# Keeping the second FFN's low weight halves in DRAM between its two passes

## The chip, the cores and the metric

One core of one Trainium2 chip runs the whole program. The metric is the time of one execution in device microseconds (us); the kernel before takes 3142.2 us, the median of three runs (3121.45 to 3152.75).

## The reference

Two layers of a decoder run over 1024 tokens of width 1024, float32. Layer 0 mixes tokens with an S5 state space model and differential attention, layer 1 with RWKV-7. Each layer ends in a gated SwiGLU FFN of hidden width 2816, and these two FFNs are what the change is about:

```python
def swiglu(h, w_gate, w_up, w_down):
    return (jax.nn.silu(h @ w_gate) * (h @ w_up)) @ w_down

for l in range(DEPTH):                       # DEPTH = 2
    ...
    h = rms_norm(x, norm_ffn[l]) * (1.0 + scale_f) + shift_f
    x = x + gate_f * swiglu(h, ffn_w_gate[l], ffn_w_up[l], ffn_w_down[l])
```

## The kernel before

The 1024 tokens are two blocks of 512 (`TB`). Each FFN makes one pass over block 0 and one over block 1, and each pass reads all three weight matrices. A pass (`ffn`, line 516) goes through the hidden width in six chunks of 3, 3, 4, 4, 4 and 4 slabs of 128 columns (`CHUNKS`, line 47). For each slab there is a gate tile and an up tile of 128x1024 (512 KB); then, for the chunk, eight down tiles d0 to d7 of 128x384 (192 KB) or 128x512 (256 KB). TensorE takes 24 matmuls of 512 columns for a gate or an up tile, and 9 or 12 for a down tile.

Each operand of these matmuls is split into a rounded high half and the rest, the low half. For a weight tile this is `wsplit` (line 443): the raw tile is loaded (line 448), ScalarE casts it to the high half (451), and the low half is raw minus high, on VectorE (457) or, when `eng` is GpSimd, there in pieces of 256 columns (464). With `key` given, the low half is instead stored to DRAM by the first pass (`flush_lo`, line 469, at the next `wsplit`) and loaded by the second (453):

```python
        nc.scalar.copy(hi, raw)
        if key in self.los:
            nc.sync.dma_start(lo.bitcast(F32), self.los.pop(key))
            return hi, lo
        self.flush_lo()
        if eng is None:
            nc.vector.tensor_tensor(lo, raw, hi.bitcast(F32), op=ALU.subtract)
        ...
        if key is not None:
            self.unsaved = key, lo, shape
```

Raw, high and low tiles have two buffers each (pool `wp`, line 182). So the high or the low half of a tile can be written only when TensorE has done with the tile two before it, while a raw tile can come as soon as its two readers have done. For each slice of 128 rows, `mm3g` (line 483) issues three matmuls: high weights by high activations, high by low, low by high. The first matmul that needs a low half is thus the third of its tile. Down tiles have one peculiarity (lines 564 to 567): d0 and d1 both run all but their last slice, then d0 and d1 finish one right behind the other, then d2 to d7 follow in turn.

The passes stand in `run` (line 1772) beside other work. Layer 0's pass over block 0 runs beside attention, with VectorE's subtraction, and stores its low halves; its pass over block 1 runs beside the RWKV algebra of block 0 and loads them. Layer 1's pass over block 0 runs beside the algebra of block 1 with the subtraction on GpSimd (`pool`, lines 1835 and 1839), its last chunk's down tiles after the output projection `rwkv_wo`. Layer 1's pass over block 1 (lines 1843 to 1848) comes last and runs alone, but for the transposes and stores of the output (`store_x`); there VectorE subtracts. TensorE's order is fixed by the program (`manual_schedule`, line 1790). The other queues, SyncE's DMA queue among them, are ordered by a scheduler, and each executes strictly in that order.

Of the kernel before, what the change touches and what calls it, by code (L numbers as in the profile page):

```python
# [18 lines left out]
P = 128  # L19
D = 1024  # L20
S = 1024
KT = D // P
# [67 lines left out]
def chain(*gens):  # L90
    for g in gens:
        yield from g


def lockstep(*gens):

    gens = list(gens)
    while gens:
        for g in gens[:]:
            if next(g, gens) is gens:  # L100
                gens.remove(g)
        yield
# [44 lines left out]
class Trunk:  # L147
# [368 lines left out]
    def ffn(self, l, st, chunks, eng=None, parts="ud", dtag="B"):  # L516

        nc, A = self.nc, self.A
        wg, wu, wd = A["ffn_w_gate"][l], A["ffn_w_up"][l], A["ffn_w_down"][l]
        gate = self.mod[l][:, 40:48]  # L520
        tp, x = self.tp, st["x"]
        hh, hl = st["h"]
        if "d" not in st:
            st["d"] = [self.page([P, 4, TB], F32R, "dd", dtag) for _ in range(2)]
        dd = st["d"]
        for f0, f1 in chunks:
            nf = f1 - f0
            for f in range(f0, f1) if "u" in parts else ():
                yield from next(self.inject, ())
                pp, gens = [], []  # L530
                for w, nme in ((wg, "pg"), (wu, "pu")):
                    hi, lo = self.wsplit(
                        w[:, f * P : (f + 1) * P].rearrange("(k p) n -> p k n", p=P), [P, KT, P], eng, None if l else (nme, f)
                    )
                    pt = self.ps.tile([P, TB], F32, tag="mm", name=self.nm(nme))
                    g = self.mm3w(pt, hi, lo, hh, hl, KT)
                    if f:
                        yield from g
                    gens.append(g)
                    pp.append(pt)  # L540
                if not f:
                    yield from lockstep(*gens)

                sg = tp.tile([P, TB], F32, tag="t0", name=self.nm("sg"))
                nc.scalar.activation(sg, pp[0], AF.Tanh, scale=0.5)
                nc.vector.scalar_tensor_tensor(sg, sg, 1.0, pp[0], op0=ALU.add, op1=ALU.mult)
                hd = tp.tile([P, TB], F32, tag="t1", name=self.nm("hd"))
                nc.vector.scalar_tensor_tensor(hd, pp[1], 0.5, sg, op0=ALU.mult, op1=ALU.mult)
                nc.scalar.copy(dd[0][:, f - f0, :], hd)
                nc.vector.tensor_tensor(dd[1][:, f - f0, :], hd, dd[0][:, f - f0, :].bitcast(F32), op=ALU.subtract)  # L550
            if "d" in parts:

                def down(n):
                    hi, lo = self.wsplit(
                        wd[f0 * P : f1 * P, n * P : (n + 1) * P].rearrange("(k p) n -> p k n", p=P), [P, nf, P], eng,
                        None if l else (f0, n),
                    )
                    pd = self.ps.tile([P, TB], F32, tag="mm", name=self.nm("pd"))
                    yield from self.mm3w(pd, hi, lo, dd[0], dd[1], nf)
                    nc.vector.scalar_tensor_tensor(x[:, n, :], pd, gate[:, n : n + 1], x[:, n, :], op0=ALU.mult, op1=ALU.add)  # L560
                    if l == 0 and f1 == NF:
                        self.square(x[:, n, :], n)

                d0, d1 = down(0), down(1)
                yield from self.some(d0, nf - 1)
                yield from self.some(d1, nf - 1)
                yield from chain(d0, d1, *(down(n) for n in range(2, KT)))
# [1350 lines left out]
```

## Time and profile before

| | us |
|---|---|
| median of three runs | 3142.2 (3152.75, 3142.2, 3121.45) |
| the profiled execution's own time | 3132.61 |
| its span, first to last instruction | 3130.8 |
| layer 1's algebra of block 1, with most of the FFN pass over block 0 | 2066 to 2640 |
| output projection, last down tiles of block 0 | 2640 to 2730 |
| layer 1's FFN pass over block 1, output stores | 2730 to 3131 |

Times in the trace count from the span's start. The page gives the busy time of each engine; idle time of an engine counts only where the end of the span hangs on it. A matmul's busy time overlaps that of the next one, so the spacing of matmul starts tells more than their durations. The granted TensorE clock is 1.00 at 2.4 GHz.

### The profile page before, as it was taken

The page shows a single profiled execution, that of the slowest core. Times are in us where ns is not written, and L with a number is a line of the kernel's source. Part 1 is how long each engine was busy: PE and PEld are TensorE (multiplying, and loading weights), DVE is VectorE, ACT ScalarE, POOL GpSimd, SP SyncE. Part 2 cuts the span into 40 slices and gives each one's busy share as a digit, 9 for nine tenths or more (in the row PEclk, how much of TensorE's full clock was granted, in tenths as well). Part 3 has the DMA queues.
Part 4 walks back from the last instruction along what each step waited for, and adds up shares of the span by engine and source line. Part 5 has one row for each costly group of instructions (what it writes and reads, how often), then busy time and mean ns, then how long its engine had stood idle before and what let it go on. Part 6 is the DMA issues. An engine that isn't in the chain of part 4 may idle for free.

```text
span 3130.8 us, 51897 instructions
## 1 busy us (share of the span) xinstructions
PE 2891.5 (92%) x19582; PEld 2232.2 (71%) x19582; DVE 1852.6 (59%) x3886; ACT 1219.5 (39%) x2542; POOL 787.4 (25%) x1127
## 2 busy tenths in 40 slices
PE   4879998998899999999999999989999999999999
PEld 1668866776677767677777777667777778777777
DVE  6854655556574744677777336467778773444443
ACT  3212444333322644454544236444444443322222
POOL 6552501001110300122221112035455545300000
PEclk7889999999999999999999999999999999999999
DMA  7764222546786445434434564422222223523333
GB/s 247 196 148 75 71 75 84 158 130 207 232 285 196 158 140 155 133 110 138 127 119 138 166 197 134 155 88 79 69 68 85 73 77 111 167 86 90 101 102 93
DMA packets 532746, 411.90 MB, mean 132 GB/s; under 512 B 47225, under 2 KB 474513, under 8 KB 531473
## 3 DMA queue, kind: packets, MB, share of 16 engines
q1 hardware_dynamic: 517168, 378.16, 40.2%
q0 software_dynamic: 7632, 25.68, 2.6%
q10 hardware_dynamic: 7696, 4.74, 0.5%
q8 instruction: 156, 2.56, 0.3%
q14 instruction: 94, 0.76, 0.1%
HBM read 331.42 MB, written 77.07 MB: 130 GB/s over the span
## 4 chain that ended last, share of the span: by engine, by line
PE 72%; DVE 12%; DMA 8%; ACT 4%; issue 3%; POOL 1%; SPq 0%; ACTq 0%; DVEq 0%; POOLq 0%
PE pu L489 14%; PE pg L489 14%; PE pd L489 12%; PE pkrv L489 8%; PE pout L489 5%; PE pq L489 4%; DMA mwt<-in_w_ada 2%; DVE wlo L457 2%; DMA ks<-kd 1%; PE sps L1027 1%; DMA wraw<-in_ffn_w_gate 1%; ACT whi L451 1%; DVE FS L1509 1%; PE pA L1536 1%; DMA wlo<-wld 1%
## 5 line engine op out<-in xcount | busy, mean ns | idle before, releaser
L451 ACT CAST whi<-wraw 128x1024 fp32r<-128x1024 f32 (+2 forms) x472 | 402.0, 852 | 934.9 <-PE pu L489 203.6
L457 DVE TENSOR_TENSOR wlo<-wraw,whi 128x1024 fp32r<-128x1024 f32 (+2 forms) x288 | 297.6, 1033 | 297.5 <-ACT whi L451 285.8
L489 PE MATMUL pd<-dd,whi 128*128 128x512 f32 x1408 | 458.4, 407 | 15.1 <-DVE x L560 10.6
L489 PE MATMUL pg<-fhi,whi 128*128 128x512 f32 x704 | 296.7, 421 | 22.4 <-ACT whi L451 13.0
L489 PEld LDWEIGHTS pd<-dd,whi 128*128 128x128 f32 x1408 | 251.8, 188 | 79.2 <-ACT whi L451 19.9
L489 PE MATMUL pu<-fhi,whi 128*128 128x512 f32 x704 | 291.9, 415 | 2.3 <-ACT ev L1393 1.6
L489 PE MATMUL pd<-dd,wlo 128*128 128x512 f32 x704 | 279.5, 397 | 8.5 <-DMA wlo<-wld 8.2
L489 PE MATMUL pg<-fhi,wlo 128*128 128x512 f32 x704 | 282.1, 401 | 2.9 <-DVE wlo L457 2.6
L489 PE MATMUL pu<-fhi,wlo 128*128 128x512 f32 x704 | 278.9, 396 | 2.6 <-DVE wlo L457 1.5
L489 PE MATMUL pg<-flo,whi 128*128 128x512 f32 x704 | 280.3, 398 | 0.0
L489 PE MATMUL pu<-flo,whi 128*128 128x512 f32 x704 | 277.5, 394 | 0.0
L464 POOL TENSOR_TENSOR wlo<-wraw,whi 128x256 fp32r<-128x256 f32 (+1 forms) x272 | 203.6, 777 | 217.4 <-ACT whi L451 212.2
L560 DVE SCALAR_TENSOR_TENSOR x<-pd,mod,x 128x512 f32<-128x512 f32 x192 | 143.5, 748 | 138.8 <-PE pd L489 137.8
L489 PE MATMUL pkrv<-xh,whi 128*128 128x512 f32 x384 | 164.9, 429 | 15.9 <-ACT ev L1393 11.2
L489 PEld LDWEIGHTS pg<-fhi,whi 128*128 128x128 f32 x704 | 134.3, 191 | 58.7 <-ACT whi L451 15.5
L489 PEld LDWEIGHTS pd<-dd,wlo 128*128 128x128 f32 x704 | 132.4, 188 | 48.5 <-DMA wlo<-wld 12.3
L489 PEld LDWEIGHTS pg<-fhi,wlo 128*128 128x128 f32 x704 | 134.2, 191 | 38.1 <-DVE wlo L457 6.2
L489 PEld LDWEIGHTS pu<-fhi,whi 128*128 128x128 f32 x704 | 132.8, 189 | 35.6 <-ACT ev L1393 2.5
L489 PEld LDWEIGHTS pu<-fhi,wlo 128*128 128x128 f32 x704 | 132.6, 188 | 34.1 <-DVE wlo L457 2.0
L489 PE MATMUL pkrv<-xh,wlo 128*128 128x512 f32 x384 | 154.9, 403 | 1.7 <-DVE wlo L457 1.7
L489 PE MATMUL pkrv<-xl,whi 128*128 128x512 f32 x384 | 154.2, 402 | 0.0
L489 PEld LDWEIGHTS pg<-flo,whi 128*128 128x128 f32 x704 | 134.7, 191 | 24.8
(460 smaller groups left out, 5933.5 us busy)
## 6 DMA issues: line engine op xcount, KB each, us to landing
wraw<-in_ffn_w_gate SPq DMA_DIRECT2D x88, 512.0 KB, 3.8
wraw<-in_ffn_w_up SPq DMA_DIRECT2D x88, 512.0 KB, 4.0
wraw<-in_ffn_w_down SPq DMA_DIRECT2D x128, 256.0 KB, 2.7
mwt<-in_w_ada POOLq DMA_DIRECT2D x48, 512.0 KB, 6.1
wld<-wlo SPq DMA_DIRECT2D x44, 512.0 KB, 3.1
wlo<-wld SPq DMA_DIRECT2D x44, 512.0 KB, 3.3
mwt<-in_w_ada SPq DMA_DIRECT2D x32, 512.0 KB, 5.9
wraw<-in_ffn_w_down SPq DMA_DIRECT2D x64, 192.0 KB, 2.4
```

What stands on the lines that cost most here:

```text
L451: nc.scalar.copy(hi, raw)
L457: nc.vector.tensor_tensor(lo, raw, hi.bitcast(F32), op=ALU.subtract)
L464: eng.tensor_tensor(o, a, h, op=ALU.subtract)
L489: nc.tensor.matmul(out, lhsT=w(k), rhs=x(k), start=first and i == 0, stop=last and i == n - 1)
L560: nc.vector.scalar_tensor_tensor(x[:, n, :], pd, gate[:, n : n + 1], x[:, n, :], op0=ALU.mult, op1=ALU.add)
L1027: nc.tensor.matmul(sp[:, c0 : c0 + n], lhsT=qT[r : r + 64, hd, o : o + P], rhs=kT[r : r + 64, hd % 2, c0 : c0 + n], start=True, stop=c0 + ...
L1509: v.scalar_tensor_tensor(FS[r, :, o : o + 64], c8(x)[r], 0.5 if x is bt else 1.0, c8(Wi)[r], op0=M, op1=M)
L1536: nc.tensor.matmul(pas[h][:, c, :], lhsT=FS[rows[h], c, :], rhs=AR[h][rows[h], c, :], start=True, stop=True)
```

## The change

The condition that kept layer 1 from having a key goes, and the layer number enters the key. Layer 1's pass over block 0 now stores each low half that GpSimd has computed; its pass over block 1 loads it instead of having VectorE subtract.

```diff
@@ ffn, gate and up tiles
-                        w[:, f * P : (f + 1) * P].rearrange("(k p) n -> p k n", p=P), [P, KT, P], eng, None if l else (nme, f)
+                        w[:, f * P : (f + 1) * P].rearrange("(k p) n -> p k n", p=P), [P, KT, P], eng, (l, nme, f)
@@ ffn, down tiles
-                        None if l else (f0, n),
+                        (l, f0, n),
```

TensorE's, GpSimd's and (but for two pairs of neighbours) ScalarE's instructions keep their order. VectorE loses 91 subtractions. The SyncE queue gains 92 stores and 91 loads. On it, at the down tiles of the last pass's first chunk, there stood before only raw loads (wraw, line 448), each behind VectorE's last reading of the raw tile two before:

```order
L448 DMA wraw_28421<-in_ffn_w_down 128x3x128 [waits DMAHW2_49,DVE_49]
L448 DMA wraw_28434<-in_ffn_w_down 128x3x128 [waits DMAHW3_49,DVE_49]
L448 DMA wraw_28455<-in_ffn_w_down 128x3x128 [waits DMAHW4_49,DVE_49]
L448 DMA wraw_28480<-in_ffn_w_down 128x3x128 [waits DMAHW5_49,DVE_49]
L448 DMA wraw_28497<-in_ffn_w_down 128x3x128 [waits DMAHW6_49,DVE_49]
```

At the same place now each raw load is followed by a load of a low half (wlo, line 453) from its DRAM copy (wld):

```order
L448 DMA wraw_28616<-in_ffn_w_down 128x3x128 [waits DMAHW3_49,Activation_49]
L453 DMA wlo_28606<-wld_20794 128x384 [waits DMAHW4_49,PE_49]
L448 DMA wraw_28637<-in_ffn_w_down 128x3x128 [waits DMAHW5_49,Activation_49]
L453 DMA wlo_28619<-wld_20875 128x384 [waits DMAHW6_49,PE_49]
L448 DMA wraw_28662<-in_ffn_w_down 128x3x128 [waits DMAHW7_49,Activation_49]
L453 DMA wlo_28640<-wld_20920 128x384 [waits DMAHW0_49,PE_49]
L448 DMA wraw_28679<-in_ffn_w_down 128x3x128 [waits DMAHW1_49,Activation_49]
```

The load of a low half waits for TensorE (PE), which must have done with the tile two before, and the raw loads now wait for ScalarE alone. In the pass over block 0, beside the algebra, the same queue had raw loads that wait for GpSimd (Pool) between the algebra's own loads and stores (ks, rr, wa, RV, g2w, zd):

```order
L448 DMA wraw_21496<-in_ffn_w_gate 128x8x128 [waits DMAHW7_49,Activation_49,Pool_49]
L1767 DMA zd<-yq_20918 128x2x128 [waits DMAHW5_49,DVE_49]
L1460 DMA ks_21395<-kd 128x2x128 [waits DMAHW6_49,DVE_49]
L448 DMA wraw_21627<-in_ffn_w_up 128x8x128 [waits DMAHW1_49,Activation_49,Pool_49]
L448 DMA wraw_21785<-in_ffn_w_gate 128x8x128 [waits DMAHW0_49,DMAHW4_49,Activation_49,Pool_49]
```

Now a store stands directly ahead of each of these raw loads and has taken over its wait for GpSimd:

```order
L473 DMA wld_21379<-wlo_21224 128x1024 [waits DMAHW2_49,Pool_49]
L448 DMA wraw_21526<-in_ffn_w_gate 128x8x128 [waits DMAHW4_49,DMAHW3_49,Activation_49]
L1767 DMA zd<-yq_20936 128x2x128 [waits DVE_49]
L1460 DMA ks_21425<-kd 128x2x128 [waits DMAHW5_49,DVE_49]
L473 DMA wld_21531<-wlo_21377 128x1024 [waits DMAHW6_49,Pool_49]
L448 DMA wraw_21659<-in_ffn_w_up 128x8x128 [waits DMAHW7_49,Activation_49]
```

The order of the algebra's transfers among the raw loads is the same as before. Since `flush_lo` stores a tile only at the next `wsplit` that computes one, the last tile of block 0 is stored under a key that the last tile of block 1 has already asked for: that one tile is still subtracted on VectorE, and its store is not used.

## Rows read from the trace of the kernel before

**Rows 1.** The page: busy time of the engines; TensorE's granted clock by slice.

```profile
PE 2891.5 (92%) x19582; PEld 2232.2 (71%) x19582; DVE 1852.6 (59%) x3886; ACT 1219.5 (39%) x2542; POOL 787.4 (25%) x1127
...
PEclk7889999999999999999999999999999999999999
```

**Rows 2.** Busy time by stage: window, length, engines (instructions), clock, DMA share, GB/s.

```profile
1228.00:1841.00 613.00, 586.76 (x5221) 448.19 (x5220) 387.67 (x1048) 274.70 (x700) 117.34 (x175) 0.99 0.45 137
2066.00:2640.00 574.00, 542.87 (x5047) 416.04 (x5046) 415.26 (x1031) 256.27 (x666) 293.54 (x411) 1.00 0.27 78
...
2730.00:3131.00 401.00, 385.01 (x1654) 304.09 (x1652) 166.30 (x219) 101.34 (x144) 0.00 (x0) 0.99 0.32 95
```

**Rows 3.** TensorE's groups, 2730 to 3131: busy, mean ns, idle before and its releaser.

```profile
L489 PE MATMUL pd<-dd,whi 128*128 128x512 f32 x356 | 113.7, 400 | 3.4 <-DVE x L560 2.2 <-DVE xo L373 1.2
L489 PE MATMUL pg<-fhi,wlo 128*128 128x512 f32 x176 | 70.7, 401 | 1.1 <-DVE wlo L457 1.1
...
L489 PE MATMUL pu<-fhi,wlo 128*128 128x512 f32 x176 | 70.1, 398 | 1.5 <-DVE wlo L457 1.5
```

**Rows 4.** VectorE's costliest group, 2730 to 3131.

```profile
L457 DVE TENSOR_TENSOR wlo<-wraw,whi 128x1024 fp32r<-128x1024 f32 (+2 forms) x92 | 84.6, 920 | 99.2 <-ACT whi L451 98.5
```

**Rows 5.** Timeline (start, length, what), last pass, first chunk: d2's subtraction and start.

```profile
2775.18 0.55 DVE L457 TENSOR_TENSOR wlo<-wraw,whi 128x384 fp32r<-128x384 f32 x1
2775.41 0.71 PE L489 MATMUL pd<-dd,whi 128*128 128x512 f32 x2 [0.24 <-DVE x L560]
```

**Rows 6.** Timeline, layer 0, block 1, last chunk: down tiles' loads (SPq) and matmuls.

```profile
1821.26 0.33 SPq L453 DMA_DIRECT2D wlo<-wld  x1
...
1824.92 0.50 PE L489 MATMUL pd<-dd,wlo 128*128 128x512 f32 x1 [1.15 <-DMA wlo<-wld]
...
1827.54 0.32 SPq L453 DMA_DIRECT2D wlo<-wld  x1
...
1828.44 0.70 PE L489 MATMUL pd<-dd,whi 128*128 128x512 f32 x2 [0.24 <-DVE x L560]
...
1830.36 0.50 PE L489 MATMUL pd<-dd,wlo 128*128 128x512 f32 x1 [1.22 <-DMA wlo<-wld]
...
1835.80 0.32 SPq L453 DMA_DIRECT2D wlo<-wld  x1
...
1838.89 0.40 PE L489 MATMUL pd<-dd,wlo 128*128 128x512 f32 x1
```

**Rows 7.** DMA issues, 1228 to 1841: count, KB each, median us to landing.

```profile
wlo<-wld SPq DMA_DIRECT2D x44, 512.0 KB, 3.3
...
wlo<-wld SPq DMA_DIRECT2D x31, 256.0 KB, 2.8
...
wlo<-wld SPq DMA_DIRECT2D x16, 192.0 KB, 2.4
...
ks<-kd SPq DMA_DIRECT2D x14, 128.0 KB, 4.0
```

**Rows 8.** Timeline, layer 0, block 1, fifth chunk: d6, gate load behind it.

```profile
1763.86 0.33 SPq L453 DMA_DIRECT2D wlo<-wld  x1
...
1764.32 0.45 SPq L448 DMA_DIRECT2D wraw<-in_ffn_w_gate  x1
...
1768.67 0.50 PE L489 MATMUL pd<-dd,wlo 128*128 128x512 f32 x1 [1.56 <-DMA wlo<-wld]
```

**Rows 9.** What the SyncE queue waited for, 2066 to 2640: total us, times, longest.

```profile
SPq L448 <- POOL wlo L464: 132.4, 67, 3.4
```

**Rows 10.** DMA issues, 2066 to 2640.

```profile
ks<-kd SPq DMA_DIRECT2D x14, 128.0 KB, 2.3
```

**Rows 11.** TensorE by stretch: window, length, busy (matmuls), granted clock, DMA share, GB/s.

```profile
2050.00:2053.50 3.50, 1.41 (x7) 1.00 0.02 9
2053.50:2057.30 3.80, 3.80 (x13) 0.55 0.93 265
...
1815.00:1831.00 16.00, 13.39 (x56) 1.00 0.57 172
```

## The prediction

> **What bounds the kernel now.** I read the page first, then the busy time by stage, then in the last stage TensorE's groups with their idle time, and last the timeline at single tiles. The page shows TensorE busy 92% of the span, its clock full outside the first slices [rows 1]. By stage, the last pass (2730 to 3131) is TensorE's alone: 385.01 us busy of 401 while VectorE has 166.30 and GpSimd nothing [rows 2]. The reader is to see there that VectorE, whose 92 subtractions go (84.6 us, [rows 4]), is not what the end waits for. TensorE's idle time that names the low half is 1.1 us before gate and 1.5 us before up matmuls, and none before down matmuls [rows 3]. So at most 2.6 us can be gained where work is taken away. The stage in which work is added, the algebra with the pass over block 0, is also TensorE's: 542.87 of 574 us [rows 2].
>
> The question is therefore whether a load can be as punctual as the subtraction was. The subtraction of a down tile takes 0.55 us and follows the cast at once; when d2 starts at 2775.41 its low half is all but there [rows 5]. A load takes 2.4 us for 192 KB, 2.8 for 256 KB and 3.3 for 512 KB from issue to landing [rows 7]. It can't be issued earlier than the subtraction could start, because the buffer it writes is the one that TensorE leaves free two tiles before.
>
> **The change part by part.** One matmul per 0.233 us is the unit (385.01 us for 1654, [rows 2]). Layer 0's pass over block 1 already does what the change asks of layer 1, and near its end, when the algebra thins out, it runs about as dense as the last pass will. I take the prices there.
>
> *Down tiles in a row, d3 to d5.* With four slices, a load is issued at 1835.80 and the third matmul of its tile comes at 1838.89 without a wait [rows 6]: the cover is 3.09 us against 2.8. This is the matmul time of one tile (12 x 0.233 = 2.80) plus two matmuls less the issue. With three slices the cover is three matmuls shorter, 3.09 - 0.70 = 2.39, against 2.4. Price: nothing. If that cover is gone because a load lands 0.4 us later, 0.4 us on every second tile, some 3 us in all.
>
> *Gate and up tiles in a row.* The cover is 24 matmuls, 5.6 us plus 0.3, against 3.3. Nothing; it would take a landing beyond 5.9 us.
>
> *From up to down tiles, six times.* d1's buffer is left by the last up tile, and only d0's nine matmuls lie between; d2's is left by d0, and only d1's last slice lies between. The rows show both waits: 1.15 us at 1824.92 for the load issued at 1821.26 (landing 3.66 us), and 1.22 us at 1830.36 for that of 1827.54 (2.82 us) [rows 6]. The 0.24 us on VectorE's residual ahead of d2 is there in both kernels [rows 5, 6], so it doesn't count. In the last pass there is less other traffic. At 2.8 us d1 would wait only 2.8 - 2.37 (9 + 2 matmuls less 0.2) = 0.43. So a turn costs between 1.65 and 2.37 us; I take 1.9, nearer to the median landing. With three slices d1 has 0.70 less cover and both loads land 0.4 sooner: 0.73 + 0.82 = 1.55, about the same. Six turns: 6 x 1.9 = 11.4 us (9.3 to 14.2).
>
> *From down to gate tiles, five times.* The raw gate and up tiles of 512 KB come in beside the low halves of d6, d7 and gate. The row has d6's load issued at 1763.86, the gate tile right behind at 1764.32, and TensorE waiting 1.56 us until 1768.67: a landing of 4.81 us [rows 8]. The gate's own low half needs 3.3 us where d7 covers 3.09: 0.2. With three slices the gate's cover is 2.39: 0.9. Three turns of 1.8 and two of 2.5 are 10.3 us. The lower bound takes the median landings for all (0.2 and 0.9: 2.4 us), the upper 4.81 us for two loads of each turn (twice 1.72 and twice 2.42: 20 us).
>
> *First gate and up pair.* They run in lockstep, so the up tile's load has five matmuls (1.2 us) of cover against 3.3: some 2.3 us, where 1.5 us went on the subtraction: +0.8 (0 to 2).
>
> *Removed.* The gate matmuls' 1.1 us [rows 3] goes; the up tile's 1.5 is counted above. VectorE's 84.6 us free nothing else, since it is idle most of that stage.
>
> *Stores in the pass over block 0.* 92 stores of 34.6 MB (44 of 512 KB, 32 of 256, 16 of 192) over some 650 us are about 53 GB/s on top of 78, under the 137 of the stage that loads them in layer 0 [rows 2]. On the SyncE queue a store waits for GpSimd's subtraction; queued behind it are the next raw load and the algebra's ks, rr, wa and RV loads, for which VectorE, ScalarE and TensorE wait. But the raw load at that place waited for the same GpSimd instruction before (132.4 us in 67 waits, [rows 9]), so the queue stands no longer than it did. GpSimd must now also wait for a store before it writes that buffer again, but that is two tiles later. What is left is traffic ahead of the ks loads: they land in 2.3 us here [rows 10] and in 4.0 us in the stage where low halves are loaded [rows 7]. Sixteen times 1.7 us, all of it exposed, is 27 us, the upper bound; below, -1. I take +2, near the side of nothing, because that layer 0 stage has its loads held up by queue entries that wait for TensorE, which the stores don't.
>
> *Last tile.* It is still subtracted, and its store of 256 KB is not on the path: nothing.
>
> Sum: 11.4 + 10.3 + 0.8 - 1.1 + 2 = +23.4 us, which is 3132.6 + 23.4 = 3156.0 on the profiled execution. That execution is 9.6 us below the median of the three runs shown. The mean of all four times is 3137.3, and from it I forecast 3160.7 us, rounded 3161.
>
> The rows say one more thing of such waits. Where TensorE was busy only 1.41 of 3.50 us, the granted clock fell to 0.55 (from 2.4 towards 1.2 GHz) over the next 3.8 us; in the 16 us that hold the two waits of rows 6 it stayed 1.00 [rows 11]. The Trainium skill, "TensorE: Matmul & The Clock Gate", section "HAM oscillation — how this bites in real kernels", describes a kernel whose DMA wait between short groups of matmuls throttles the clock anew each time. By that rule every turn would pay a stretch at half clock; by the row of the nearest case none would. It is a rival below.
>
> **The rivals.**
>
> *Hidden after all (-3 to +8 us).* The landings of rows 6 and 8 were stretched by the algebra's own transfers; alone, d1 waits 0.4 us, and the turns to gate almost nothing. Against it: d2's 1.22 us came with a plain landing of 2.82 us, so six of these (7.3 us) remain. About 3142 us.
>
> *Every down tile late, slower than before.* In the last pass the traffic roughly doubles from 95 GB/s [rows 2], and if the down tiles' loads land in 4.81 us throughout, as d6's did [rows 8], the cover fails on every second tile, as a late tile lengthens its successor's cover. Sixteen of the 32 four-slice tiles by 1.72 and eight of the 16 three-slice ones by 2.42 are 46.9; with +0.8 - 1.1 + 2 that is +48.6, 3186 us. It decides from a landing of about 3.2 us on. For it: 4.81 was seen. Against: no wait at the tiles of 1831 to 1841.
>
> *The clock falls at the turns, slower.* If each of the 11 turns is followed by 3.8 us at 0.55, each costs 3.8 x 0.45 = 1.7 us, 18.8 more: +42, 3179 us. For it: the fall after the gap at 2050. Against: the full clock across the two waits of rows 6.
>
> *The algebra's loads suffer, slower.* The upper bound of the stores: +23.4 - 2 + 27 = +48, 3186 us. Against: the wait that the store takes over.
>
> *The change doesn't do what it says.* The key could miss; but the queue shows 91 loads and VectorE 91 subtractions fewer, so only the last tile misses. No chance of its own.
>
> **How the numbers follow.** Within 1% means within 31 us of 3137, about what a measurement of this kernel can tell from no change. My forecast has 0.54, of which 0.43 lie under +31 and 0.11 above. Hidden after all has 0.17, every tile late 0.17, the clock 0.06, the algebra's loads 0.04. Something that makes TensorE faster than its 2.6 us of removable waits allow has 0.02. Slower: 0.11 + 0.17 + 0.06 + 0.04 = 0.38; same: 0.43 + 0.17 = 0.60; faster 0.02. The range leaves out the bottom of the hidden case and the tail above +56: 3136 to 3193. The forecast's own range, from its terms' bounds without the algebra's 27 us, is 3147 to 3178 (9.3 + 2.4 + 0 - 1.1 - 1 = 9.6 above 3137.3, and 14.2 + 20 + 3 + 2 - 1.1 + 2 = 40).
>
> **What would show it.** In the changed kernel's profile, TensorE's idle time before down matmuls with the low half should name the load (wlo from wld) with 12 to 20 us in the last pass, in two waits of about 1 us at d1 and d2 of each chunk, and the gate matmuls should name it with 1 to 5. VectorE's subtraction keeps one instruction there. The granted clock stays 0.99 or 1.00, and the pass over block 0 takes the same time within 3 us. I am wrong if d3 to d5 wait too, if the clock falls behind the turns, if ks lands near 4 us and the stage from 2066 grows, or if TensorE doesn't wait for the loads at all.

## The result, and the profile after

The changed kernel takes 3160.41 us, the median of 20 runs (3142.47 to 3168.86), against 3137.41 us of 20 runs of the kernel before on the same chip. The ratio is 1.0071, 95% interval 1.0059 to 1.0083: 19 to 26 us slower, and by the bound of 1% no change. The forecast was 3161 us.

The profiled execution took 3150.99 us, its span 3149.1. That is 18.3 us over the profiled one before, a little under the interval, so a few of the timed microseconds have no place in the pair of traces.

The page of the changed kernel answers to [rows 1]. VectorE has 91 instructions and 77.6 us fewer, and TensorE has 12 us more busy time for the same 19582 instructions. The down matmuls with the low half, of both layers together, waited 8.2 us for loads before, all in layer 0's pass over block 1, and wait 14.8 now.

```profile
PE 2903.3 (92%) x19582; PEld 2236.4 (71%) x19582; DVE 1775.0 (56%) x3795; ACT 1219.6 (39%) x2542; POOL 788.2 (25%) x1127
...
PEclk7889998999999999999999999999999999999999
...
L457 DVE TENSOR_TENSOR wlo<-wraw,whi 128x1024 fp32r<-128x1024 f32 (+2 forms) x197 | 213.1, 1082 | 197.4 <-ACT whi L451 194.3
...
L489 PE MATMUL pd<-dd,wlo 128*128 128x512 f32 x704 | 281.4, 400 | 15.5 <-DMA wlo<-wld 14.8
```

The busy time by stage, with the columns of [rows 2]: the algebra's stage, and the last pass from its first to its last matmul.

```profile
2066.00:2640.00 574.00, 541.99 (x5028) 414.90 (x5028) 414.08 (x1029) 254.87 (x664) 293.66 (x411) 0.99 0.43 130
2731.60:3143.40 411.80, 389.00 (x1649) 301.80 (x1647) 88.13 (x124) 100.16 (x142) 0.00 (x0) 1.00 0.58 172
```

The last pass took 394.1 us before (2731.0 to 3125.1) and takes 411.7 now: 17.6 of the 18.3 us are here. Of the 14.8 us above, 9.2 are this pass's and 5.6 layer 0's, so layer 0's 8.2 fell by 2.6 though the change leaves that pass as it was. From 1228 to 1841 these waits are 3.4 to 6.6 us in the profiled executions of before, after and the runs below, so this is no effect of the change that could be told from chance. The algebra's stage carries 130 instead of 78 GB/s and TensorE does the same work in it (541.99 against 542.87 us). Inside the last pass I split the time at each change from up to down matmuls and back. The down phases of the six chunks grew by 2.95, 2.98, 1.49, 2.77, 1.43 and 1.87 us, 13.5 together; the gate and up phases by 4.1.

TensorE's groups in the last pass, as in [rows 3]:

```profile
L489 PE MATMUL pd<-dd,whi 128*128 128x512 f32 x352 | 112.2, 400 | 3.4 <-DVE x L560 2.2 <-DVE xo L373 1.2
L489 PE MATMUL pd<-dd,wlo 128*128 128x512 f32 x177 | 71.4, 403 | 9.6 <-DMA wlo<-wld 9.2
L489 PE MATMUL pg<-fhi,wlo 128*128 128x512 f32 x176 | 71.0, 403 | 3.8 <-DMA wlo<-wld 3.8
L489 PE MATMUL pu<-fhi,wlo 128*128 128x512 f32 x176 | 70.4, 400 | 2.8 <-DMA wlo<-wld 2.8
```

In the kernel before, the down matmuls with the low half have this row, from 2730 to 3131:

```profile
L489 PE MATMUL pd<-dd,wlo 128*128 128x512 f32 x178 | 70.0, 393 | 0.0
```

They waited for nothing before; now for 9.6 us, of which 9.2 are put down to the load. The gate's 1.1 us of VectorE have become 3.8 us of the load, the up tile's 1.5 have become 2.8. Where [rows 4] had 92 subtractions, VectorE's groups of the same stretch have one, the last tile's:

```profile
L457 DVE TENSOR_TENSOR wlo<-wraw,whi 128x512 fp32r<-128x512 f32 x1 | 0.7, 681 | 0.0
```

The timeline of the first turn from up to down tiles shows the two waits of a turn (the stretch that [rows 5] touched):

```profile
2773.36 0.34 SPq L453 DMA_DIRECT2D wlo<-wld  x1
...
2774.55 0.63 PE L489 MATMUL pd<-dd,whi 128*128 128x512 f32 x2
...
2775.89 0.50 PE L489 MATMUL pd<-dd,wlo 128*128 128x512 f32 x1 [0.71 <-DMA wlo<-wld]
...
2776.23 0.63 PE L489 MATMUL pd<-dd,whi 128*128 128x512 f32 x2
...
2777.83 0.34 SPq L453 DMA_DIRECT2D wlo<-wld  x1
...
2778.73 0.70 PE L489 MATMUL pd<-dd,whi 128*128 128x512 f32 x2 [0.24 <-DVE x L560]
...
2780.36 0.50 PE L489 MATMUL pd<-dd,wlo 128*128 128x512 f32 x1 [0.92 <-DMA wlo<-wld]
```

d1's load goes out at 2773.36, as the last up tile leaves the buffer, and d1 needs it 1.66 us later (2774.55 plus two matmuls of 0.233). It starts at 2775.89. d2's load goes out at 2777.83 and its need comes at 2779.2; it starts at 2780.36. Each load took 2.53 us, which is a plain landing:

```profile
wld<-wlo SPq DMA_DIRECT2D x41, 512.0 KB, 3.1
...
ks<-kd SPq DMA_DIRECT2D x14, 128.0 KB, 2.8
...
wlo<-wld SPq DMA_DIRECT2D x43, 512.0 KB, 3.5
...
wlo<-wld SPq DMA_DIRECT2D x31, 256.0 KB, 2.8
...
wlo<-wld SPq DMA_DIRECT2D x16, 192.0 KB, 2.5
```

These are issues of two stages, with their median times to landing: the first two rows from 2066 to 2640, the others from the last pass. They answer to [rows 7] (3.3, 2.8, 2.4 us) and [rows 10] (ks 2.3 us).

The same rows show what a wait costs. From 2774.55 to 2776.23 lie three matmuls, 0.70 us at the usual pace, and they took 1.68: 0.98 us lost where the row says 0.71. The printed idle time starts at a modelled end 0.17 us behind the pace of 0.233 (a row is 0.40 long), and the next matmul comes 0.34 us after the late one. So each wait costs about 0.27 us over its row; worked out in the same way, every wait for a low half in this pass gives 0.26 to 0.28. Twelve waits of 9.2 us are then 12.5 of the down phases' 13.5 us.

### The profile page after: what moved, and what is told of

The parts are those of the page before. It is cut to its first block, busy times and chain, and to the rows that moved or that the text cites. A ratio compares the mean times of both kernels' runs of the same rounds, so it can differ in the third digit from the quotient of the medians.

```text
span 3149.1 us, 52131 instructions
## 1 busy us (share of the span) xinstructions
PE 2903.3 (92%) x19582; PEld 2236.4 (71%) x19582; DVE 1775.0 (56%) x3795; ACT 1219.6 (39%) x2542; POOL 788.2 (25%) x1127
## 4 chain that ended last, share of the span: by engine, by line
PE 72%; DVE 11%; DMA 9%; ACT 4%; issue 2%; POOL 0%; SPq 0%; ACTq 0%; DVEq 0%; POOLq 0%
PE pu L489 14%; PE pg L489 14%; PE pd L489 11%; PE pkrv L489 8%; PE pout L489 5%; PE pq L489 3%; DMA wlo<-wld 3%; PE sps L1027 1%; DVE wlo L457 1%; ACT whi L451 1%; DMA ks<-kd 1%; DMA mwt<-in_w_ada 1%; DMA wraw<-in_ffn_w_gate 1%; DVE FS L1509 1%; PE pA L1536 1%
## 5 line engine op out<-in xcount | busy, mean ns | idle before, releaser
L457 DVE TENSOR_TENSOR wlo<-wraw,whi 128x1024 fp32r<-128x1024 f32 (+2 forms) x197 | 213.1, 1082 | 197.4 <-ACT whi L451 194.3
L489 PE MATMUL pd<-dd,wlo 128*128 128x512 f32 x704 | 281.4, 400 | 15.5 <-DMA wlo<-wld 14.8
L546 DVE SCALAR_TENSOR_TENSOR sg<-sg,pg 128x512 f32<-128x512 f32 x88 | 60.2, 684 | 173.2 <-ACT sg L545 172.7
```

The source lines that it names most:

```text
L489: nc.tensor.matmul(out, lhsT=w(k), rhs=x(k), start=first and i == 0, stop=last and i == n - 1)
```

## The experiments

All were timed beside the kernel before, in five rounds each. Phases of the last pass are taken from the timeline of each profiled execution, as above; "up" is the sum of the gate and up phases.

| kernel | ratio to before, 95% interval | last pass us | up, against before | down, against before |
|---|---|---|---|---|
| before | 1 | 394.1 | | |
| changed kernel | 1.0071 [1.0059, 1.0083] | 411.7 | +4.1 | +13.5 |
| 1 stores only | 1.0000 [0.9987, 1.0014] | 394.2 | 0.0 | +0.2 |
| 2 gate and up only | 1.0051 [1.0033, 1.0070] | 414.5 | +20.3 | +0.1 |
| 3 down only | 1.0057 [1.0037, 1.0077] | 405.8 | -1.8 | +13.5 |
| 4 three buffers | 0.9993 [0.9981, 1.0004] | 387.7 | -5.8 | -0.6 |
| 5 gate and up only, GpSimd's queue | 1.0066 [1.0051, 1.0081] | 416.3 | +22.1 | +0.1 |
| 6 before with three buffers | 0.9998 [0.9986, 1.0011] | 393.7 | -0.3 | -0.1 |
| 7 d0's last slice sooner | 1.0048 [1.0032, 1.0065] | 408.7 | +6.5 | +8.2 |
| 8 gate and up only, three buffers | 1.0003 [0.9988, 1.0019] | 388.7 | -5.4 | 0.0 |
| 9 three buffers again | 0.9991 [0.9974, 1.0009] | 389.2 | -4.2 | -0.7 |

**1. The stores alone.** Everything is stored, nothing loaded; the last pass subtracts as before.

```
-  ... eng, (l, nme, f)
+  ... eng, None if l and eng is None else (l, nme, f)
-  (l, f0, n),
+  None if l and eng is None else (l, f0, n),
```

> The pass over block 0 stores its low halves as in the changed kernel; the last pass subtracts them on VectorE as before, so nothing reads the stores. Theory (the loads come too late for their short cover at the chunks' turns): the stores cost 0 to 4 us, so 0 to +4 us against the kernel before, and the last pass takes its 394 us from first to last matmul again. Rival (the stores hold up the algebra, and the last pass's extra time in one profile is by chance): +15 to +22 us, in the stretch from 2066 to 2640.

Measured 1.0000 (-4 to +4 us). The ks loads land in 2.9 us:

```profile
ks<-kd SPq DMA_DIRECT2D x14, 128.0 KB, 2.9
```

The stores cost nothing that can be measured. SyncE's queue does wait for GpSimd longer than in [rows 9], at the store's line:

```profile
SPq L473 <- POOL wlo L464: 276.1, 67, 12.3
```

In the kernel before, the same view has another row that the raw loads waited on; here it is down to 1.1 us:

```profile
SPq L448 <- ACT whi L451: 172.6, 52, 10.1
```

So on these two the queue stood 305 us before (172.6 + 132.4), and at the store's line it stands 276 now: the store takes over both waits.

**2. Gate and up tiles alone** (the down tiles subtracted).

```
-  (l, f0, n),
+  None if l else (l, f0, n),
```

> Low halves of gate and up tiles are stored and loaded, those of down tiles subtracted as before. Theory (cover): the six down phases of the last pass fall back to the kernel before's lengths (13.5 us of the 17.6 us go), the gate and up phases keep about 4 us; with the stores +4 to +8 us against before. Rival (traffic makes all loads late, so the cost goes with the bytes): two thirds of the bytes remain, so about +12 us of the last pass, +13 to +16 in all.

Measured +16 us (10 to 22), which is the rival's total and not the theory's +4 to +8. The stretches fit neither: the down phases did fall back (+0.1 us instead of +13.5), as the theory had it, but the up phases grew by 20.3 us, where it had about 4 and the rival about 12 for the whole pass. The first gate tile of five chunks waits 2.52, 2.92, 2.92, 2.27 and 1.03 us. The timeline at the second chunk:

```profile
2785.13 0.37 SPq L448 DMA_DIRECT2D wraw<-in_ffn_w_up  x1
2785.99 0.34 SPq L453 DMA_DIRECT2D wlo<-wld  x1
...
2788.26 0.40 PE L489 MATMUL pg<-flo,whi 128*128 128x512 f32 x1
...
2791.18 0.49 PE L489 MATMUL pg<-fhi,wlo 128*128 128x512 f32 x1 [2.52 <-DMA wlo<-wld]
```

The low half goes out 0.86 us behind the raw up tile and takes 5.2 us. The windows of this kernel (columns as in [rows 2]) say why, and show a second cost:

```profile
2788.00:2791.20 3.20, 0.68 (x4) 0.24 (x3) 0.75 (x1) 1.04 (x1) 0.00 (x0) 1.00 1.01 336
2791.20:2795.00 3.80, 3.80 (x16) 3.09 (x17) 0.00 (x0) 0.00 (x0) 0.00 (x0) 1.00 0.95 301
...
2846.00:2851.50 5.50, 5.46 (x13) 4.30 (x14) 0.00 (x0) 0.00 (x0) 0.00 (x0) 0.50 0.56 182
```

During the wait the DMA engines are wholly busy (1.01) at 336 GB/s: several transfers share them. Behind this wait the clock stays at 1.00; behind the next, of 2.92 us until 2846.04, it is granted at 0.50 (1.2 instead of 2.4 GHz) for 5.5 us. There are four such stretches, of 3.4, 3.2, 5.6 and 6.0 us by the starts of the matmuls. Against the pace of 0.233 they lose 8.4 us together; the kernel before has one, which loses 1.6, so 6.8 us are new. The seven waits for loads hold 15.7 us and cost 0.27 more each, 17.5; the three waits for VectorE's low halves, which cost 3.4 before, are gone, and the one for VectorE's sg (its part of the gate's activation) is 1.47 instead of 2.06. So 17.5 - 3.4 - 0.6 + 6.8 = 20.3 us, what the up phases grew by.

**3. Down tiles alone.**

```
-  ... eng, (l, nme, f)
+  ... eng, None if l else (l, nme, f)
```

> Low halves of down tiles are stored and loaded, those of gate and up tiles subtracted as before. Theory (cover): the waits at d1 and d2 of each chunk stay, those at d6 and d7 shrink since no gate or up low half is loaded beside them, and the gate phases are as before: the down phases are 9 to 14 us longer than before, +10 to +16 us in all. Rival (cost goes with the bytes): a third of them remain, +6 us of the last pass, +7 to +9 in all.

Measured +18 us (12 to 24), a little over the +10 to +16 expected and far from the rival's +7 to +9; the last pass +11.7, and the down phases +13.5 as in the changed kernel. TensorE's groups in its last pass:

```profile
L489 PE MATMUL pd<-dd,wlo 128*128 128x512 f32 x177 | 71.4, 403 | 9.4 <-DMA wlo<-wld 9.4
L489 PE MATMUL pg<-fhi,wlo 128*128 128x512 f32 x176 | 70.5, 401 | 0.0
```

So the waits at down tiles are the down tiles' own; loads for gate and up tiles are not needed for them. Nor does the cost go with the bytes: runs 2 and 3 add up to +34 us, the whole change to +22, and in the traces their last passes to 32.1 us against 17.6. Of the 14.5 us between, 6.8 are run 2's slow stretches. The rest is seen at the turn that run 2 shows. In the changed kernel the wait at d7 (0.51 us, with its surplus 0.78) comes before the gate tile, so the gate's low half goes out 2.67 us ahead of the gate's first matmul (2792.01 and 2794.68) instead of 1.93 (2785.99 and 2787.92); it lands in 4.4 us instead of 5.2, and TensorE waits 1.07 us instead of 2.52. No wait at a turn is longer than 1.4 us there, and none of the turns shows a slow clock.

**4. Three buffers for the low halves in the last pass**, in the room that the algebra's pool leaves. Nothing else is changed.

```
+  self.close(self.ap)
+  self.ap = self.lop = self.open("m1w", 3, side="right")
...
-  lo = self.wp.tile(shape, F32R, tag="wlo", ...)
+  lo = (self.lop or self.wp).tile(shape, F32R, tag="wlo", ...)
```

> The changed kernel with three buffers for low halves in the last pass, in the space that the algebra's tiles leave. Theory (cover): a load can go out one whole tile earlier, so TensorE's waits for low halves in the last pass go from about 15 us to under 3; against the kernel before -1 to +5 us (the stores' 0 to 4 remain, the subtraction's 2.6 us of waits go). Rival (landing): with the traffic of the last pass doubled the loads are late wherever they are issued, and at least half of the 17.6 us remains: +11 to +20 us.

Measured 0.9993 (-6 to +1 us), the last pass 24 us shorter than in the changed kernel and 6.4 shorter than before. TensorE's groups, and the landings of the same loads:

```profile
L489 PE MATMUL pd<-dd,wlo 128*128 128x512 f32 x180 | 70.9, 394 | 0.0
...
L489 PE MATMUL pg<-fhi,wlo 128*128 128x512 f32 x176 | 69.6, 395 | 0.1
```

```profile
wlo<-wld SPq DMA_DIRECT2D x41, 512.0 KB, 3.5
...
wlo<-wld SPq DMA_DIRECT2D x31, 256.0 KB, 2.7
...
wlo<-wld SPq DMA_DIRECT2D x16, 192.0 KB, 2.5
```

The loads take as long as in the changed kernel and move no fewer bytes; only their issue is sooner, and the waits are gone. The short cover is the cause, not the landing. Of the 6.4 us, 1.6 come from the slow stretch of the kernel before, which is gone as well.

**5. Run 2 with the loads of the low halves on GpSimd's queue.**

```
-  nc.sync.dma_start(lo.bitcast(F32), self.los.pop(key))
+  (nc.gpsimd if key[0] == 1 else nc.sync).dma_start(lo.bitcast(F32), self.los.pop(key))
```

> The kernel in which only the gate and up tiles' low halves are stored and loaded, with the last pass's loads of them issued by GpSimd, idle there, instead of SyncE. In the kernel with the loads on SyncE's queue, the first gate tile of a chunk waited 2.5 to 2.9 us, because its load, issued 0.9 us behind the up tile's raw load of 512 KB, took 5.2 us to land; the up phases of the last pass were 20.2 us longer than before. Theory A (one queue serves its transfers in order, so the low half moves only when the raw tiles ahead of it have gone): on its own queue it lands in 3.3 to 4 us, the waits at gate fall to 0.5 to 1.3 us each, the up phases are 3 to 10 us longer than before instead of 20, ratio 1.000 to 1.003. Theory B (the 16 engines are shared, whichever queue a transfer stands in): it lands in 4.4 us or more, the waits stay at 2 us or more, ratio 1.004 to 1.007. Under both the raw up tile lands no sooner than now. If a load issued by GpSimd has a longer start of its own than one of SyncE, also the tiles within a chunk would wait, which the trace would show as waits at every second gate or up tile.

Measured 1.0066. The wait stays, on a queue with nothing ahead of the load:

```profile
2795.63 0.37 SPq L448 DMA_DIRECT2D wraw<-in_ffn_w_up  x1
2796.75 0.54 POOL L453 DMA_DIRECT2D wlo<-wld  x1 [26.97 <-PE pd L489]
...
2801.62 0.50 PE L489 MATMUL pg<-fhi,wlo 128*128 128x512 f32 x1 [2.30 <-DMA wlo<-wld]
```

4.87 us from issue to use, where SyncE's queue had 5.19, and the five gate tiles wait 1.4 to 2.7 us. Theory A's landing of 3.3 to 4 us and its waits of 0.5 to 1.3 are not met, the ratio and most waits are theory B's: the order of SyncE's queue is not what makes the landing long. That the engines' rate makes it long is argued, not shown by this run alone: they are at 0.91 of their time and 273 GB/s here (2796.7 to 2801.7), and GpSimd's loads take longer in the median as well (3.8 us against 3.4 in run 2), so some 0.4 of the 4.87 us may be that queue's own. In run 2 the engines were full. The Trainium skill, "DMA: Bandwidth & Descriptors", section "Where 436 GB/s comes from", puts the limit of transfers between HBM and SBUF at about 358 GB/s per core; the 336 GB/s of run 2 with all engines busy agree with a bound of that size.

**6. The kernel before with three buffers** (the edit of run 4).

> The kernel before, with three instead of two buffers for the low halves in its last pass and nothing else: no stores, no loads. Theory (the 6.4 us that the last pass of the change with three buffers was shorter than before come from the loads, which take away VectorE's subtractions and with them the waits on the low half, on the square root's and residual's turn on VectorE and so on; a third buffer for a subtraction that follows its cast at once is worth nothing): the last pass takes 393 to 395 us, ratio 0.999 to 1.001, TensorE still waits some 2.6 us for VectorE's low half at gate and up tiles. Rival (the third buffer alone gives it, and the loads give nothing): last pass 387 to 390 us, ratio 0.998 to 0.999, no such waits.

Measured 0.9998, last pass 393.7: the theory. The waits on VectorE are all still there:

```profile
L489 PE MATMUL pg<-fhi,wlo 128*128 128x512 f32 x176 | 70.3, 400 | 1.1 <-DVE wlo L457 1.1
...
L489 PE MATMUL pu<-fhi,wlo 128*128 128x512 f32 x176 | 69.7, 396 | 1.5 <-DVE wlo L457 1.5
```

A third buffer alone gives nothing, so what the last pass gains in run 4 takes both the loads and the buffer.

**7. d0's last slice ahead of d1's last two**, in the changed kernel's last pass.

```
-  yield from self.some(d1, nf - 1)
+  yield from self.some(d1, nf - 2 if l and eng is None else nf - 1)
```

> The changed kernel with one slice moved in TensorE's order at each turn of the last pass: d0's last slice comes ahead of d1's last two slices instead of between its last and last but one. So d0's buffer comes free three matmuls (0.70 us) sooner before d2 needs its low half, and nothing else is changed. Theory (each wait is the load's landing less the matmuls between the buffer's release and its need): d2's waits, 0.92, 0.91, 1.02, 1.22 and 1.19 us in the changed kernel, fall by 0.7 to 0.2 to 0.5 us; d1's stay at 0.2 to 0.8; the down phases sum to 10 to 8.5 us over the kernel before instead of 13.5; ratio 1.004 to 1.007. Rival (the landing is late because of the traffic at the turn, and a sooner issue only makes it queue longer): d2's waits stay at 0.9 to 1.2. A second rival: the last slice of the hidden values is late for d0 when it comes sooner, and a wait on VectorE's or ScalarE's dd takes the place of d2's.

Measured 1.0048 (the interval overlaps the changed kernel's), the down phases +8.2 instead of +13.5. d2's waits fell, but by 0.09 to 0.35 us and not by 0.7. The first turn:

```profile
2779.21 0.34 SPq L453 DMA_DIRECT2D wlo<-wld  x1
...
2780.42 0.63 PE L489 MATMUL pd<-dd,whi 128*128 128x512 f32 x2
...
2781.63 0.50 PE L489 MATMUL pd<-dd,wlo 128*128 128x512 f32 x1 [0.58 <-DMA wlo<-wld]
```

Counted from d0's first matmul, the load goes out 0.76 us sooner than in the changed kernel (3.91 against 4.67) and takes 2.42 us. But d2 begins 0.45 us sooner too (5.12 against 5.57): the 0.24 us that it waited for VectorE's residual of d0 is gone as well. So the cover grew by 0.3 us only, from 1.37 to 1.68, and it did so at each of the five turns at which d2 waited, while the landings stayed at 2.4 to 2.8 us: against the rival, a sooner issue did not lengthen them. The cover rule (wait = landing less cover, less the 0.17 us by which the row reads short) holds to 0.1 us; the expectation had left the residual out. Of the 5.3 us that the down phases gained, waits for loads are 1.8 and the residual's five waits 2.4 with their surplus; those five were in the kernel before as well, and the same edit there was not tried. The up phases took 2.3 us more than in the changed kernel, 1.6 of it in a second slow stretch, behind waits of 1.46 and 0.53 us at the first chunk's second gate tile.

**8. Run 2 with three buffers.**

> The kernel in which only the gate and up tiles' low halves are stored and loaded, with three instead of two buffers for low halves in the last pass. With two buffers its last pass took 414.3 us (before 394.1): the first gate tile of five chunks waited 2.52, 2.92, 2.92, 2.27 and 1.03 us, and behind some of these waits TensorE ran at the half clock for 3 to 6 us. Theory (cover: the load is issued when the buffer comes free, and a third buffer lets it be issued a whole down tile earlier, 2.8 us with four slices, 2.1 with three; the stretches at half clock come from the waits): all waits on the loads fall to under 0.5 us, at most one stretch at half clock is left near the start of the pass, the last pass takes 387 to 391 us, ratio 0.998 to 1.000. Rival (the landing is what fails, since three transfers of 512 KB share the engines there: sooner issue only means slower landing): waits of 1 to 2 us stay at the first gate tiles, last pass 397 to 405 us, ratio 1.001 to 1.004.

Measured 1.0003, last pass 388.7: the theory, though the 5.4 us by which the pass is shorter than before don't show in the timed ratio [0.9988, 1.0019]. TensorE waits 0.3 us in all for these loads, and no stretch at half clock is left in the pass:

```profile
L489 PE MATMUL pg<-fhi,wlo 128*128 128x512 f32 x176 | 69.6, 396 | 0.3 <-DMA wlo<-wld 0.3
```

At the second chunk the load is issued a tile sooner, still needs 5.2 us to its use, and TensorE waits 0.27 us for it where it waited 2.52:

```profile
2789.23 0.34 SPq L453 DMA_DIRECT2D wlo<-wld  x1
...
2794.43 0.50 PE L489 MATMUL pg<-fhi,wlo 128*128 128x512 f32 x1 [0.27 <-DMA wlo<-wld]
```

So at this turn the landing is as long as in run 2, and costs 0.27 us instead of 2.52.

**9. Run 4 again.**

> The changed kernel with three instead of two buffers for low halves in the last pass, the same text as the run that gave a ratio of 0.9993, timed again to see whether it beats the kernel before: its last pass was 6.4 us shorter than before, 0.2% of the time. Theory (that is gained and nothing is given back elsewhere): ratio 0.997 to 0.999. Rival (the stores in the pass over block 0, some 35 MB, give part of it back): ratio 0.999 to 1.001.

Measured 0.9991, on the border of theory and rival, and the interval holds 1. Its last pass was 4.9 us shorter than before, with two waits for loads at gate tiles, of 0.81 and 0.60 us. That this version beats the kernel before is not shown; it takes back what the change cost.

## Why the prediction was right, and where its steps were off

The total was right: +23.4 forecast, +22 timed (19 to 26). Against the pair of traces (+18.3) the sum is 5 us too high. The mechanism is the one named, a load whose buffer comes free too late for its landing, and runs 3, 4, 7 and 8 show it from several sides. The terms were less good than their sum: two were too large, others too small, and that the forecast came within 1 us of the timed median is luck.

*From up to down tiles, 11.4.* The three-slice turns came as worked out: 0.71 and 0.67 at d1 against 0.73, 0.92 and 0.91 at d2 against 0.82. At the four-slice turns d2 was as forecast in three of four (1.02, 1.22, 1.19 against 1.22) and did not wait in one. But d1 waited only once, 0.24, where about 0.7 of the 1.9 were for it: the lower price of 0.43, from a plain landing, was nearer. Idle time of the six turns: 6.9 us.

*From down to gate tiles, 10.3.* This term was oversized (and 3 x 1.8 + 2 x 2.5 is 10.4). I took the wait of 1.56 us from [rows 8], with its landing of 4.81, in every turn, and one at gate besides. Measured were 0.51, 0.37 and 1.08 at d7 and 1.07, 1.38, 0.19 and 0.29 at gate: 4.9 us.

*What a wait costs.* Both terms took the printed idle time as the price (1.22 at d2, 1.56 at the end of the chunk). The 0.27 us that each wait costs beyond it were missing: for the 15 waits of the turns 4.1 us. So the turns really took 9.0 (6.9 + 8 x 0.27) and 6.8 us (4.9 + 7 x 0.27) of the 11.4 and 10.3, and this error made up for part of the two above.

*d3 to d5, nothing.* Right but for one wait of 0.40 us at a d4.

*First pair, +0.8.* The up tile waited 2.78 instead of 1.55, +1.2, and the second gate tile, which I had not counted, 0.82, while its wait for VectorE's sg fell from 2.06 to 1.47. The first chunk's up phase grew by 1.7 us. The gate's 1.1 us of VectorE did go; run 3 shows that it goes with the down tiles' subtractions alone.

*Stores, +2.* Run 1 has none, within 4 us, and the reason given holds, though with 172.6 us of ScalarE's wait that I had not counted beside GpSimd's 132.4.

**The rivals.** Hidden after all: no, 9.2 us of waits at down tiles. Every down tile late: no, the median landings stayed at 2.5 and 2.8 us while the traffic went from 94 to 172 GB/s. d3's loads, issued 0.9 us behind d2's, did take 3.6 to 4.3 us in four chunks, more than the 3.2 from which this rival was to decide; but d2's wait comes ahead of their use, and TensorE did not wait for them. The algebra's loads: ks went from 2.3 to 2.8 us, not to 4.0, and run 1, where they take 2.9, costs nothing for it. The clock: the changed kernel has one slow stretch, behind the first pair's wait, and the turns have none.

```profile
2736.30:2740.00 3.70, 3.70 (x10) 2.88 (x11) 0.00 (x0) 0.00 (x0) 0.00 (x0) 0.54 0.14 40
...
2835.00:2840.00 5.00, 3.85 (x16) 2.59 (x15) 1.87 (x3) 1.02 (x2) 0.00 (x0) 1.00 0.58 157
```

The second row holds d2's wait in the second turn. The kernel before has one slow stretch too, behind a wait of 2.06 us for VectorE, so the clock is no part of the difference:

```profile
2746.70:2750.10 3.40, 3.33 (x8) 2.65 (x9) 2.45 (x4) 0.62 (x1) 0.00 (x0) 0.51 0.68 194
```

Of what the profile was to show, two things came out otherwise: 9.2 us before down matmuls, not 12 to 20, and not two waits in each chunk: d1 waited in three of the six and d2 in five. The gate's 3.8 lie in the 1 to 5 named.

## What to carry to other kernels

Before a computed operand is replaced by a load, write down for each tile when its buffer is released and when it is first needed; the difference, in matmuls of the tiles between, has to exceed the landing, and it is smallest where tiles are interleaved or change in size. When it fell short here, one more buffer was the remedy (run 4), not fewer loads (runs 2 and 3) or another queue (run 5). Price each wait a little above its idle row, 0.27 us here, and look at the clock in the stretch behind it.

## What was not expected of the hardware

A load's landing depended on what moved beside it. 512 KB took 3.4 to 3.5 us in the median on SyncE's queue, and 4.4 to 5.2 us beside raw tiles at the turns to the gate, on either queue, with the 16 engines at 0.91 to 1.01 of their time and 273 to 336 GB/s.

A wait of some 2 to 3 us can cost its length again: the two stretches behind run 2's waits of 2.92 us lost 2.6 and 2.8 us. In run 2 the clock went to 0.50 behind waits of 2.92, 2.92 and 3.11 us and not behind 2.52 or 2.27, and once behind two shorter ones in a row (1.47 and 0.88); in run 5 it fell behind one of 2.21 and not behind one of 2.30; in run 7 it fell behind 1.46 and 0.53 in a row, and in the changed kernel not behind 1.47 and 0.82 at the same place. Length alone doesn't decide it, and what does stays open. The Trainium skill, "TensorE: Matmul & The Clock Gate", section "HAM oscillation — how this bites in real kernels", tells of a kernel that is throttled anew by each wait for a DMA; run 2 shows that pattern at two of the five gate tiles, the changed kernel's shorter waits at none of its turns.
